# A decoder trunk on one core: fourteen pairs of up products instead of twelve, and the first down group ahead of the pairs

## The chip, the core and the metric

The kernel runs on one core of one Trainium2 chip. The metric is the device time of one execution in microseconds (us), shown as the median of several runs. A profile of one execution gives, for each engine, what it did and when: PE is TensorE (matmuls; PEld is its weight load), DVE is VectorE, ACT is ScalarE, POOL is GpSimd, and SP issues most of the DMAs.

## The reference, cut to what matters

Two layers of a decoder trunk for 512 positions of width 1024. In each layer three groups of heads (differential attention, a short convolution, RWKV-7 time mixing) share a norm, one input projection and one output projection; a squared-ReLU MLP follows. The change lies in the MLP alone:

```python
h = rms_norm(x, norm_mlp_g[l])
x = x + jnp.square(jax.nn.relu(h @ w_mlp_up[l])) @ w_mlp_down[l]    # 1024 -> 4096 -> 1024
```

## The kernel before, in words

**Layout.** Everything is transposed: a tile has 128 features as partitions and the 512 positions as its columns, so `x` is 8 tiles of 128x512. Weights come from HBM as `raw` tiles of 128x512 (four blocks of 128x128, 256 KB).

**Precision.** A product in fp32 precision is made of three passes of fp32r matmuls. Each operand is split into a high part (ACT casts it: `whi`, `mh`, `shi`, `thi`) and a low part (a subtraction of the two: `wlo`, `ml`, `slo`, `tlo`); the passes are hi by hi, hi by lo and lo by hi. So each tile that goes into a matmul first needs one cast on ACT and one subtraction with two inputs in SBUF on DVE or POOL.

**The MLP of a layer.** 32 groups of 128 up features. Up products come in two kinds:

- A single group, `up(i)`: 8 blocks by 3 passes, 24 matmuls of 512 columns, into one PSUM tile. Groups 0 to 2 are multiplied at the end of the mixing stage; `up` then only squares them.
- A pair, `two(i0, i1)`: two groups together by a scheme with 7 products of half size in place of 8. Each product is 12 matmuls of 256 columns, 84 in all. It needs 4 `raw` tiles, sums of them on DVE (`s1` to `s4`, line 1461), a cast (line 1455) and a subtraction (line 1456) for each of the 7 products, with five buffers in the ring of `shi` and `slo`. On the other side it needs sums of blocks of the normed input, `thi` and `tlo`.

The sums of blocks are made once a layer. `by_gain(j)` (ACT, line 1427) scales `x[j]` into `bn[j]`; `blocks(k)` takes `bn[k]` and `bn[k+4]`, makes four sums of 128x256 on DVE (lines 1433 to 1436) in two tiles `t[0]`, `t[1]`, casts each on ACT (`thi`, line 1440) and subtracts (`tlo`, line 1441). The tiles `t` take turns in four buffers, `s1` and `s2` for even `k`, `s3` and `s4` for odd `k`; so block 2 overwrites what block 0 used, and the pairs' own sums use the same four names.

Each up group is then squared by `square`: DVE scales the PSUM tile by the norm and cuts it at zero (`r`, line 1400), ACT squares it (`m`, line 1402), `kept` casts it (`mh`, ACT, line 1391) and subtracts on POOL (`ml`, line 1392). These are the "mids", in a ring of 10.

Down products, `down(h, js)`: a group `h` takes four mids and adds their part to `x[j]`; each `dn` tile is 12 matmuls of 512 columns, and DVE adds it to `x[j]` (line 1516). There are 8 groups of 8 tiles in a layer; the last layer does its last two in another way (`dnF`).

**Order.** The mixing stage is issued in an order that is written out by hand. The MLP is written as a plain program, and a scheduler puts it into an order for each engine; every engine then works through its own list strictly in order and waits for semaphores. The program's order before is: groups 0 to 7 single, with a `by_gain` pair and a `blocks` after each of the groups 4 to 7; the whole first down group; then twelve pairs, each followed by half a down group.

Of the kernel before, what the change touches and what calls it, by code (L numbers as in the profile page):

```python
# [10 lines left out]
F32 = mybir.dt.float32  # L11
# [5 lines left out]
ALU = mybir.AluOpType  # L17
# [7 lines left out]
NK = D // P  # L25
# [150 lines left out]
         "wp/wlo 01201201201201202102102102102102102102102102102102102102102102102102102102 ")  # L176
NG = NG_IN + NG_OUT + NG_UP + NG_DN

N_ONE = 8

WHOLE = 5
PT = 1
N_TWO = (NG_UP - N_ONE) // 2
MID = tuple(range(N_ONE)) + tuple(N_ONE + i + N_TWO * j for i in range(N_TWO) for j in range(2))

# [83 lines left out]
def tile_trunk(ctx: ExitStack, tc: tile.TileContext, xT, wts, prm_d, cst_d, lora_d, gup_d, lam_d, fin_d, out):  # L269
    nc = tc.nc  # L270
    act, dve, pool = nc.scalar, nc.vector, nc.gpsimd
# [27 lines left out]
    def psum(tag, bufs, name):  # L299
        return ps.tile([P, 512], F32, tag=tag, bufs=bufs, name=name)  # L300
# [56 lines left out]
    def mm3(out_ps, w, acts, n=NK):  # L357
        for _ in mm3_steps(out_ps, w, acts, n):
            pass
# [209 lines left out]
    for l in range(L):  # L569
# [807 lines left out]
        with ExitStack() as mx:  # L1377
# [42 lines left out]
            def by_gain(j):  # L1420

                if j == 0:
                    fp.tile([P, 8], F32, tag="pad0", name=f"pad0_{l}")
                bn[j] = fp.tile([P, 2, H], F32, tag="shi" if j < 4 else "slo", bufs=5, name=f"bn{l}_{j}")
                if j == 4:
                    fp.tile([P, 24], F32, tag="pad1", name=f"pad1_{l}")
                act.activation(bn[j].rearrange("p a s -> p (a s)"), x[j], AF.Identity, scale=pr[:, C_GMLP + j:C_GMLP + j + 1],
                               bias=none)

            def blocks(k):  # L1430
                b1, b2 = bn[k], bn[k + 4]
                t = [fp.tile([P, 2, H], F32, tag=f"s{2 * (k % 2) + i + 1}", name=f"t{l}_{k}_{i}") for i in range(2)]
                dve.tensor_tensor(t[0][:, 0], b1[:, 1], b1[:, 0], ALU.subtract)
                dve.tensor_tensor(t[0][:, 1], b2[:, 1], t[0][:, 0], ALU.subtract)
                dve.tensor_tensor(t[1][:, 0], b2[:, 1], b1[:, 1], ALU.subtract)
                dve.tensor_tensor(t[1][:, 1], b2[:, 0], t[0][:, 1], ALU.subtract)
                hi, lo = th[k] = [fp.tile([P, 4, H], F32R, tag=f"t{p}{k}", name=f"t{p}{l}_{k}") for p in ("hi", "lo")]
                for i in range(2):
                    u = slice(2 * i, 2 * i + 2)
                    act.copy(hi[:, u], t[i])  # L1440
                    dve.tensor_tensor(lo[:, u], t[i], hi[:, u].bitcast(F32), ALU.subtract)

            def two(i0, i1):

# [65 lines left out]
            def down(h, js):  # L1510

                g, k0 = h // 2, 4 * (h % 2)
                for j in js:
                    pt = psum("mm", 2, f"dn{l}_{h}_{j}")
                    mm3(pt, weights(wbase + NG_IN + NG_OUT + NG_UP + 8 * g + j, k0, k0 + 4), mids[4 * h:4 * h + 4], 4)
                    dve.tensor_tensor(x[j], pt, x[j], ALU.add)  # L1516
                    if h == 2 * N_KG - 1 and j < NK - LATE:
                        norm_tile(j, f"m{l + 1}")


            for i in range(N_ONE):
                up(i)
                if i >= N_ONE - 4:
                    k = i - N_ONE + 4
                    by_gain(k)
                    by_gain(k + 4)
                    blocks(k)
            down(0, range(NK))
            h, half = 1, 0
            for p in range(N_TWO):  # L1530
                two(N_ONE + p, N_ONE + N_TWO + p)
                if len(mids) >= 4 * h + 6 and h < 2 * N_KG - 2 * (l == L - 1):
# [75 lines left out]
```

## Time and profile before

| what | value |
|---|---|
| time, median of 3 runs | 1242.42 us (1241.35 to 1243.07) |
| span of the profiled execution | 1241.5 us |
| granted TensorE clock, mean | 0.998 |
| PE busy | 1230.0 us (99%) |
| DVE busy | 912.1 us (73%) |
| ACT busy | 675.0 us (54%) |
| POOL busy | 368.0 us (30%) |

Times below are us from the start of the profiled span. A row of the timeline has start, duration, engine, line, operation, the tile written and the tiles read, partitions by columns, and in brackets how long the engine had been idle before it and what ended that. PE's matmuls overlap, so the pace of a run of them is read from start to start, not from the duration of one. In a row of the groups the numbers behind the bar are the busy time of the group, the mean duration of one in ns, and the idle time before them with what ended most of it.

### The profile page before, as it was taken

The page shows a single profiled execution, that of the slowest core. Times are in us where ns is not written, and L with a number is a line of the kernel's source. Part 1 is how long each engine was busy: PE and PEld are TensorE (multiplying, and loading weights), DVE is VectorE, ACT ScalarE, POOL GpSimd, SP SyncE. Part 2 cuts the span into 40 slices and gives each one's busy share as a digit, 9 for nine tenths or more (in the row PEclk, how much of TensorE's full clock was granted, in tenths as well). Part 3 has the DMA queues.
Part 4 walks back from the last instruction along what each step waited for, and adds up shares of the span by engine and source line. Part 5 has one row for each costly group of instructions (what it writes and reads, how often), then busy time and mean ns, then how long its engine had stood idle before and what let it go on. Part 6 is the DMA issues. An engine that isn't in the chain of part 4 may idle for free.

```text
span 1241.5 us, 24974 instructions
## 1 busy us (share of the span) xinstructions
PE 1230.0 (99%) x9492; PEld 1055.0 (85%) x9492; DVE 912.1 (73%) x1776; ACT 675.0 (54%) x1410; POOL 368.0 (30%) x457
## 2 busy tenths in 40 slices
PE   9999999999999999999999999999999999999997
PEld 6888888888899998989887888888888999998987
DVE  6787888868767676765766777887687767676753
ACT  6785655548445454544464657464583445454542
POOL 1263637342311111111026355464231211111111
PEclk9999999999999999999999999999999999999999
DMA  6523324142433333321235244332433333333121
GB/s 216 163 87 99 105 96 111 53 153 85 136 102 98 107 94 106 99 85 44 69 106 164 79 118 119 89 83 73 158 102 120 102 102 98 107 94 107 55 68 68
DMA packets 84695, 127.90 MB, mean 103 GB/s; under 512 B 21472, under 2 KB 25568, under 8 KB 84576
## 3 DMA queue, kind: packets, MB, share of 16 engines
q1 hardware_dynamic: 83568, 125.64, 33.1%
q8 instruction: 74, 1.21, 0.4%
q10 hardware_dynamic: 1008, 0.68, 0.2%
q14 instruction: 45, 0.37, 0.1%
HBM read 117.11 MB, written 9.18 MB: 102 GB/s over the span
## 4 chain that ended last, share of the span: by engine, by line
PE 93%; ACT 2%; DVE 2%; DMA 1%; POOL 1%; issue 1%; ACTq 0%; POOLq 0%; DVEq 0%
PE dn L282 25%; PE pj L282 20%; PE pa L282 11%; PE po L282 8%; PE up L282 7%; PE pb L282 6%; PE dnF L282 4%; PE pc L282 3%; PE sc L282 1%; DMA raw<-wts 1%; PE ptt L287 1%; PE pg L282 1%; PE pyy L282 1%; PE pzw L282 1%; PE pst L282 1%
## 5 line engine op out<-in xcount | busy, mean ns | idle before, releaser
L1392 POOL TENSOR_TENSOR ml<-m,mh 128x512 fp32r<-128x512 f32 x64 | 108.9, 1716 | 481.0 <-ACT mh L1391 340.6
L344 ACT CAST whi<-raw 128x512 fp32r<-128x512 f32 x142 | 87.4, 619 | 162.4 <-PE dn L282 152.8
L282 PE MATMUL dn<-mh,whi 128*128 128x512 f32 x448 | 174.8, 390 | 0.1
L282 PE MATMUL dn<-ml,whi 128*128 128x512 f32 x448 | 174.6, 390 | 0.0
L282 PE MATMUL dn<-mh,wlo 128*128 128x512 f32 x448 | 174.5, 390 | 0.0
L683 POOL TENSOR_TENSOR wlo<-raw,whi 128x512 fp32r<-128x512 f32 x84 | 111.0, 1321 | 213.1 <-ACT whi L671 175.4
L282 PE MATMUL pj<-ahim,whi 128*128 128x512 f32 x392 | 156.7, 400 | 0.4 <-DVE vf L1278 0.4
L282 PE MATMUL pj<-ahim,wlo 128*128 128x512 f32 x392 | 156.4, 399 | 0.0
L282 PE MATMUL pj<-alom,whi 128*128 128x512 f32 x392 | 155.9, 398 | 0.0
L1516 DVE TENSOR_TENSOR x<-dn,x 128x512 f32<-128x512 f32 x112 | 77.3, 690 | 103.1 <-PE dn L282 103.1
L671 ACT CAST whi<-raw 128x512 fp32r<-128x512 f32 x142 | 87.6, 617 | 83.3 <-PE pj L282 25.1
L345 DVE TENSOR_TENSOR wlo<-raw,whi 128x512 fp32r<-128x512 f32 x142 | 115.0, 811 | 11.2 <-ACT whi L344 8.3
L282 PEld LDWEIGHTS dn<-mh,wlo 128*128 128x128 f32 x448 | 84.1, 188 | 17.8
L282 PEld LDWEIGHTS dn<-mh,whi 128*128 128x128 f32 x448 | 84.1, 188 | 17.5 <-issue 0.4
L282 PEld LDWEIGHTS dn<-ml,whi 128*128 128x128 f32 x448 | 84.1, 188 | 16.7
L1455 ACT CAST shi_p<-s 128x512 fp32r<-128x512 f32 x96 | 59.6, 621 | 70.1 <-PE pa L282 55.1
L282 PEld LDWEIGHTS pj<-ahim,whi 128*128 128x128 f32 x392 | 73.9, 188 | 14.1 <-issue 0.8
L282 PEld LDWEIGHTS pj<-alom,whi 128*128 128x128 f32 x392 | 73.9, 188 | 13.9 <-issue 0.5
L282 PEld LDWEIGHTS pj<-ahim,wlo 128*128 128x128 f32 x392 | 73.9, 188 | 13.8 <-issue 0.2
L1456 DVE TENSOR_TENSOR slo_p<-s,shi_p 128x512 fp32r<-128x512 f32 x96 | 67.9, 708 | 19.7 <-ACT shi_p L1455 17.2
L282 PE MATMUL pa<-tlo,shi_p 128*128 128x256 f32 x288 | 81.3, 282 | 0.0
L282 PE MATMUL pa<-thi,shi_p 128*128 128x256 f32 x288 | 81.2, 282 | 0.0
(414 smaller groups left out, 3208.1 us busy)
## 6 DMA issues: line engine op xcount, KB each, us to landing
raw<-wts SPq DMA_DIRECT2D x389, 256.0 KB, 2.7
qs<-dqhi SPq DMA_DIRECT2D x24, 128.0 KB, 3.7
ks<-dkhi SPq DMA_DIRECT2D x24, 128.0 KB, 3.7
x<-xT SPq DMA_DIRECT2D x8, 256.0 KB, 4.6
dqhi<-qhi SPq DMA_DIRECT2D x6, 256.0 KB, 3.4
dqlo<-qlo SPq DMA_DIRECT2D x6, 256.0 KB, 3.4
dkhi<-khi SPq DMA_DIRECT2D x6, 256.0 KB, 2.7
dklo<-klo SPq DMA_DIRECT2D x6, 256.0 KB, 3.5
```

Source lines behind the costliest of these rows:

```text
L282: ins = nc.tensor.matmul(*a, **k)
L287: ins = nc.tensor.transpose(*a, **k)
L344: act.copy(hi[:, :n], raw[:, :n])
L345: (pool if a and lean[0] else dve).tensor_tensor(lo[:, :n], raw[:, :n], hi[:, :n].bitcast(F32), ALU.subtract)
L671: yield act.copy(hi[:, k0:k1], raw[:, k0:k1])
L683: yield eng.tensor_tensor(lo[:, k0:k1], raw[:, k0:k1], hi[:, k0:k1].bitcast(F32), ALU.subtract)
L1392: pool.tensor_tensor(lo, m, hi.bitcast(F32), ALU.subtract)
L1455: act.copy(hi, src)
L1456: dve.tensor_tensor(lo, src, hi.bitcast(F32), ALU.subtract)
L1516: dve.tensor_tensor(x[j], pt, x[j], ALU.add)
```

## The change

The number of single groups, `N_ONE`, goes from 8 to 4, so the number of pairs a layer goes from 12 to 14. The low parts of the block sums, `tlo`, are subtracted on POOL instead of DVE. All eight `by_gain` come right behind group 3, and the first down group follows at once, two tiles at a time, with one `blocks` after each two; the pairs start behind it.

```diff
-N_ONE = 8
+N_ONE = 4
...
                     act.copy(hi[:, u], t[i])
-                    dve.tensor_tensor(lo[:, u], t[i], hi[:, u].bitcast(F32), ALU.subtract)
+                    pool.tensor_tensor(lo[:, u], t[i], hi[:, u].bitcast(F32), ALU.subtract)
...
             for i in range(N_ONE):
                 up(i)
-                if i >= N_ONE - 4:
-                    k = i - N_ONE + 4
-                    by_gain(k)
-                    by_gain(k + 4)
-                    blocks(k)
-            down(0, range(NK))
+            for j in range(NK):
+                by_gain(j)
+            for k in range(4):
+                down(0, (2 * k, 2 * k + 1))
+                blocks(k)
             h, half = 1, 0
             for p in range(N_TWO):
                 two(N_ONE + p, N_ONE + N_TWO + p)
```

The condition behind each pair (half a down group once the mids reach `4 * h + 6`) is the same. With four mids at the start instead of eight, it is first met after the third pair, so the first three pairs of a layer follow each other directly; before, the first half group came after the first pair.

What the scheduler makes of it shows at three places, all at the start of layer 0's MLP (names: layer, then group, block or down tile; the last number only tells tiles apart).

POOL, the low parts of the first mids. Before:

```order
L1392 TENSOR_TENSOR ml0_0_4157<-m0_0_4154,mh0_0_4156 128x512
L1392 TENSOR_TENSOR ml0_1_4165<-m0_1_4162,mh0_1_4164 128x512
L1392 TENSOR_TENSOR ml0_2_4173<-m0_2_4170,mh0_2_4172 128x512
L1392 TENSOR_TENSOR ml0_3_4218<-m0_3_4215,mh0_3_4217 128x512
L1392 TENSOR_TENSOR ml0_4_4263<-m0_4_4260,mh0_4_4262 128x512
```

Now:

```order
L1392 TENSOR_TENSOR ml0_2_4173<-m0_2_4170,mh0_2_4172 128x512
L1441 TENSOR_TENSOR tlo0_0_4286<-t0_0_0_4279,thi0_0_4285 128x512
L1441 TENSOR_TENSOR tlo0_0_4286<-t0_0_1_4280,thi0_0_4285 128x512
L1441 TENSOR_TENSOR tlo0_1_4338<-t0_1_0_4331,thi0_1_4337 128x512
L1441 TENSOR_TENSOR tlo0_1_4338<-t0_1_1_4332,thi0_1_4337 128x512
L1441 TENSOR_TENSOR tlo0_2_4390<-t0_2_0_4383,thi0_2_4389 128x512
L1392 TENSOR_TENSOR ml0_3_4218<-m0_3_4215,mh0_3_4217 128x512
```

Five subtractions of the block sums stand between the third and the fourth mid's low part, where there was nothing. In layer 1 there are four.

DVE, around the squaring of group 3 (`r0_3`). Before:

```order
L345 TENSOR_TENSOR wlo39_0_4288<-raw39_0_4285,whi39_0_4287 128x512
L1441 TENSOR_TENSOR tlo0_1_4340<-t0_1_1_4334,thi0_1_4339 128x512
L1441 TENSOR_TENSOR tlo0_2_4401<-t0_2_0_4394,thi0_2_4400 128x512
L1400 SCALAR_TENSOR_TENSOR r0_3_4213<-up0_3_4176,rsf0_4108 128x512
L1441 TENSOR_TENSOR tlo0_2_4401<-t0_2_1_4395,thi0_2_4400 128x512
L345 TENSOR_TENSOR wlo39_4_4306<-raw39_4_4303,whi39_4_4305 128x512
```

Now:

```order
L345 TENSOR_TENSOR wlo66_0_4243<-raw66_0_4240,whi66_0_4242 128x512
L1433 TENSOR_TENSOR t0_2_0_4383<-bn0_2_4226 128x256
L1434 TENSOR_TENSOR t0_2_0_4383<-bn0_6_4235,t0_2_0_4383 128x256
L345 TENSOR_TENSOR wlo68_0_4295<-raw68_0_4292,whi68_0_4294 128x512
L1435 TENSOR_TENSOR t0_2_1_4384<-bn0_6_4235,bn0_2_4226 128x256
L1400 SCALAR_TENSOR_TENSOR r0_3_4213<-up0_3_4176,rsf0_4108 128x512
L345 TENSOR_TENSOR wlo69_0_4315<-raw69_0_4312,whi69_0_4314 128x512
L1436 TENSOR_TENSOR t0_2_1_4384<-bn0_6_4235,t0_2_0_4383 128x256
L1433 TENSOR_TENSOR t0_3_0_4435<-bn0_3_4228 128x256
L1435 TENSOR_TENSOR t0_3_1_4436<-bn0_7_4237,bn0_3_4228 128x256
```

Two of block 2's sums (`t0_2_0`, `t0_2_1`) now stand ahead of `r0_3`. They write the buffers that POOL's first two `tlo` read, and wait for POOL.

PE, behind group 3. Before:

```order
L282 MATMUL up0_3_4176<-ahif0_7_4061,wlo37_4_4198 128x512
L282 MATMUL up0_4_4221<-ahif0_0_3851,whi38_0_4224 128x512
L282 MATMUL up0_4_4221<-alof0_0_3852,whi38_0_4224 128x512
L282 MATMUL up0_4_4221<-ahif0_0_3851,wlo38_0_4225 128x512
L282 MATMUL up0_4_4221<-ahif0_1_3880,whi38_0_4224 128x512
```

Now, the rows from the last of the first nine matmuls of `dn0_0_0` on (the nine take mids 0 to 2):

```order
L282 MATMUL dn0_0_0_4239<-mh0_2_4172,wlo66_0_4243 128x512
L282 MATMUL dn0_0_1_4259<-mh0_0_4156,whi67_0_4262 128x512
L282 MATMUL dn0_0_1_4259<-ml0_0_4157,whi67_0_4262 128x512
L282 MATMUL dn0_0_1_4259<-mh0_0_4156,wlo67_0_4263 128x512
L282 MATMUL dn0_0_1_4259<-mh0_1_4164,whi67_0_4262 128x512
L282 MATMUL dn0_0_0_4239<-mh0_3_4217,whi66_0_4242 128x512
L282 MATMUL dn0_0_1_4259<-ml0_1_4165,whi67_0_4262 128x512
L282 MATMUL dn0_0_0_4239<-ml0_3_4218,whi66_0_4242 128x512
```

PE goes from group 3 straight into the down group: 13 matmuls on mids 0 to 2, then one that needs `mh0_3`, one more, and then one that needs `ml0_3`. In layer 1 it is 15 instead of 13.

## The prediction

> **What bounds the kernel now.** First the page's busy times and the chain of waits, then the chain in the stretch where the change lies.
>
> ```profile
> PE 1230.0 (99%) x9492; PEld 1055.0 (85%) x9492; DVE 912.1 (73%) x1776; ACT 675.0 (54%) x1410; POOL 368.0 (30%) x457
> PE 93%; ACT 2%; DVE 2%; DMA 1%; POOL 1%; issue 1%; ACTq 0%; POOLq 0%; DVEq 0%
> 289.84 35.62 PE up L282 x157
> 325.46 21.77 PE dn L282 x96
> ```
>
> PE sets the end. At the start of layer 0's MLP it runs 157 up matmuls and then the 96 of the first down group without a wait: everything that DVE, ACT and POOL do there is hidden. So two questions decide: how much PE work goes, and whether PE now waits anywhere.
>
> **What PE saves.** From the timeline of PE, the starts of group 3, group 4, the first down tile, the first pair, and the down tile behind it:
>
> ```profile
> 298.10 0.39 PE L282 MATMUL up<-ahif,whi 128*128 128x512 f32 x1
> 303.54 0.39 PE L282 MATMUL up<-ahif,whi 128*128 128x512 f32 x1
> 325.30 0.39 PE L282 MATMUL dn<-mh,whi 128*128 128x512 f32 x1
> 347.07 0.28 PE L282 MATMUL pa<-ahif,shi_p 128*128 128x256 f32 x1
> 357.07 0.40 PE L282 MATMUL dn<-mh,whi 128*128 128x512 f32 x1
> ```
>
> A single group takes 303.54 - 298.10 = 5.44 us (24 matmuls, 0.227 each), a pair 10.00 us (84 matmuls, 0.119 each). A pair replaces two singles: 2 x 5.44 - 10.00 = 0.88 us. Two more pairs in each of two layers save 4 x 0.88 = **3.5 us**. The down products only move, and the bytes stay the same: two singles and one pair both load four tiles of 256 KB. That DVE loses the `tlo` gives nothing by itself, since DVE has 2% of the chain.
>
> **The new wait, what POOL costs.** Until now group 3's mid had four more single groups, 21.8 us, before the first down tile asked for it. Now the down group stands right behind group 3, at 303.54. After 13 matmuls on mids 0 to 2 (13 x 0.227 = 2.95, so at 306.5) PE needs `mh` of mid 3, and two matmuls later `ml` of mid 3. And POOL, which makes `ml`, gets five `tlo` ahead of it. Rows of groups and of POOL's timeline:
>
> ```profile
> L1392 POOL TENSOR_TENSOR ml<-m,mh x64: 1286/1644/4517, 293.3 to 1188.9; 128x512 fp32r<-128x512 f32 x64
> L1441 DVE TENSOR_TENSOR tlo<-t,thi 128x512 fp32r<-128x512 f32 x16 | 10.5, 677 | 0.0
> 568.19 2.55 POOL L1392 TENSOR_TENSOR ml<-m,mh 128x512 fp32r<-128x512 f32 x2 [16.86 <-ACT mh L1391]
> ```
>
> `tlo` took 0.68 us on DVE. The trace has no `tlo` on POOL, but `ml` has the same form: alone, two in 2.55 us, 1.27 each; at worst 4.5. What makes the difference is DVE:
>
> ```profile
> 308.57 4.28 POOL L1392 TENSOR_TENSOR ml<-m,mh 128x512 fp32r<-128x512 f32 x1 [4.52 <-ACT mh L1391]
> 311.62 0.67 DVE L1400 SCALAR_TENSOR_TENSOR r<-up,rsf 128x512 f32<-128x512 f32 x1
> 312.22 1.18 DVE L345 TENSOR_TENSOR wlo<-raw,whi 128x512 fp32r<-128x512 f32 x1
> 359.62 3.39 POOL L1392 TENSOR_TENSOR ml<-m,mh 128x512 fp32r<-128x512 f32 x2 [28.84 <-ACT mh L1391]
> 360.68 1.19 DVE L345 TENSOR_TENSOR wlo<-raw,whi 128x512 fp32r<-128x512 f32 x1
> ```
>
> From 308.57 DVE ran subtractions back to back, and POOL's operation ended only after DVE came to `r` at 311.62, which reads PSUM; the `wlo` behind that took 1.18 instead of 0.68. At 360.68 it is DVE that waits: its `wlo` ends 0.56 us after POOL's first operation, and POOL's second comes after it. I read this as turns: an operation with two inputs in SBUF excludes the other engine's, a waiting one goes in next, and a string without a gap keeps the other out. POOL's turn, net, is 1.27 less a lead of about 0.12, so 1.15 us. The Trainium skill says the same in "SBUF — State Buffer", section "SBUF: two separate sides": DVE and GpSimd share a port pair that is locked for a whole instruction, and the loser blocks fully; the trace agrees (1.18 against 0.68).
>
> **The wait in layer 0, step by step.** Paces from the timelines, start to start:
>
> ```profile
> 290.69 0.82 ACT L1427 ACTIVATE bn<-x,none,prm 128x512 f32<-128x512 f32 x1 [0.22 <-DVE none L1418]
> 291.41 0.62 ACT L1402 ACTIVATE m<-r 128x512 f32<-128x512 f32 x1
> 292.64 0.61 ACT L1391 CAST mh<-m 128x512 fp32r<-128x512 f32 x1
> 293.15 0.62 ACT L344 CAST whi<-raw 128x512 fp32r<-128x512 f32 x1
> 299.34 0.41 DVE L1435 TENSOR_TENSOR t<-bn,bn 128x256 f32<-128x256 f32 x1
> 299.68 0.68 DVE L1400 SCALAR_TENSOR_TENSOR r<-up,rsf 128x512 f32<-128x512 f32 x1
> 300.28 0.68 DVE L345 TENSOR_TENSOR wlo<-raw,whi 128x512 fp32r<-128x512 f32 x1
> ```
>
> On ACT a `bn` takes 0.72, a cast or square 0.52; on DVE an operation of 512 columns 0.60, of 256 columns 0.34. Until 290.69 nothing changes.
>
> - ACT: eight `bn` and six casts or squares stand ahead of mid 2's square: 8 x 0.72 + 6 x 0.52 = 8.9, to 299.6. Square, `whi`, `mh`: 1.7, so `mh` of mid 2 is there at 301.3.
> - POOL: `ml` of mid 2 to 302.8, the first `tlo` to 304.1. DVE stands since about 301.7: its `t0_2_0` overwrites what that `tlo` reads. Behind it in DVE's list wait `wlo68` and `r0_3`, and for `r0_3` ACT and then PE.
> - Turns: DVE `t0_2_0` (0.4); POOL second `tlo` (1.15); DVE three operations (1.3), which reaches `r0_3` at 307.0; POOL third `tlo`, to 308.2; DVE `wlo69` and two `t` (1.3); POOL fourth, to 310.6; DVE four (1.7); POOL fifth, to 313.4; DVE `s1` (0.6); POOL `ml` of mid 3, to 315.2.
> - ACT: `r0_3` ends at 307.6; square, `shi`, `mh` make 309.3.
>
> PE stands from 306.5 to 309.3, does two matmuls (0.45), and stands to 315.2: **8.2 us** in all. Behind it PE's list is only late; the down group's weights and the pair's operands use the time.
>
> **Layer 1.** There POOL has four `tlo` ahead, and PE 15 matmuls. Group 3 starts here at 907.50 and ends at:
>
> ```profile
> 907.50 0.39 PE L282 MATMUL up<-ahif,whi 128*128 128x512 f32 x1
> 912.95 0.39 PE L282 MATMUL up<-ahif,whi 128*128 128x512 f32 x1
> ```
>
> PE runs out at 912.95 + 15 x 0.227 = 916.35. Mid 2 can't be scaled before group 2 ends (907.7); `r` to 908.4, then on ACT a `bn`, the square, a `bn` and the cast give `mh` at 910.9. Turns: `ml` to 912.3; DVE two `wlo` (1.1); POOL first `tlo` to 914.6; DVE `t0`, `r` at 915.0; POOL to 916.2; DVE two `wlo` and three `t` (2.2); POOL to 919.5; DVE one `t` (0.5); POOL to 921.1; DVE two `t` (0.8); `ml` of mid 3 to 923.1. PE stands 923.1 - 916.35 - 0.45 = **6.3 us**.
>
> Bounds for both: with no exclusion, POOL's operations one behind the other, 301.4 + 7 x 1.27 = 310.3 and 911.0 + 6 x 1.27 = 918.6, so 3.4 and 1.8 us, 5.2 together. Above, with every POOL operation at 4.5 us, it would be 26 and 21; but the strings that DVE has here are at most 2.2 us long, so I take the turns: 14.5.
>
> **TensorE's clock.** A gap of that length has a second price. PE's first rows, its last one, and two windows around the end:
>
> ```profile
> 1.22 4.18 PE L282 MATMUL idle<-zero 128*128 128x512 bf16 x10 [1.22 <-DVE zero L394]
> 5.05 0.58 PE L282 MATMUL pj<-ahim,whi_s 128*128 128x512 f32 x1
> 1235.18 0.66 PE L282 MATMUL prbF<-eyeF,rloF 128*128 128x128 f32 x4
> 1233.00:1236.00 3.00, 1.89 (x12) 1.56 (x12) 1.22 (x8) 1.14 (x5) 0.44 (x1) 1.00 0.75 261
> 1236.00:1239.00 3.00, 0.00 (x0) 0.00 (x0) 1.73 (x6) 0.25 (x1) 1.41 (x2) 0.70 0.66 229
> ```
>
> PE's last work ends at 1235.84 after some thin us, and in the next window the granted clock is down to 0.70. At the start ten matmuls took 3.83 us where 2.27 is the warm pace, 1.6 us lost. So each gap costs nothing more or about 1.6; I count one: **+1.6**. The Trainium skill, "TensorE: Matmul & The Clock Gate", section "Part 1: The HAM clock gate", halves the clock after one idle window of about 3.4 us; by it both gaps pay, which is a rival below. The end of this trace agrees as far as it goes.
>
> **The three pairs in a row.** DVE has to make a pair's operands in a pair's time: 12 operations of 0.60 and 6 of 0.34, 9.2 of 10.00 us. Rows for two pairs that follow each other at the end of layer 1, and for loads:
>
> ```profile
> 1166.11 0.28 PE L282 MATMUL pa<-ahif,shi_p 128*128 128x256 f32 x1
> 1176.11 0.28 PE L282 MATMUL pa<-ahif,shi_p 128*128 128x256 f32 x1
> 1186.17 0.40 PE L282 MATMUL dnF<-mh,whi 128*128 128x512 f32 x1
> 303.50:325.30 21.80, 21.80 (x98) 18.02 (x97) 21.75 (x34) 14.61 (x26) 10.15 (x4) 1.00 0.41 125
> ```
>
> They keep 10.00. Three take 12 tiles of 256 KB in 30 us on SP's queue, 105 GB/s, under the 125 that the last row shows with PE full. The ring of five, filled during the down group, covers the rest: I cost it at 0, and without that cover at two `ml` turns a pair, 9.2 + 2.3 - 10.0 = 1.5, times six pairs 9.
>
> **Sum.** -3.5 + 8.2 + 6.3 + 1.6 = +12.6. The profiled 1241.5 becomes 1254.1; the median of the runs lies 0.9 above the profiled span, so **1255.0**.
>
> **The rivals.**
>
> - *No exclusion:* POOL's operations keep 1.27 us, PE stands 5.2 us: -3.5 + 5.2 = +1.7, 1244.1. For it: the median `ml` is only 1.64. Against it: the 1.18 and 4.28 above.
> - *The clock falls in both gaps:* 1.6 more, 1256.6. For it: both gaps are longer than the thin stretch at the end. Against it: two matmuls divide each.
> - *Hidden after all, faster:* the mid arrives before PE asks, and 3.5 us stay: 1238.9. The place is POOL between 301.4 and 307; seven operations fit only under 0.8 us each. Against it: of 64 `ml` none took less than 1.286.
> - *DVE becomes the bound in the three pairs as well:* up to 9 more, 1259 to 1264. For it: 9.2 of 10.00 leaves little. Against it: the tail pairs keep pace, with a lighter DVE, and PE's new gap gives DVE a lead.
>
> **How the numbers follow.** Two runs of this kernel can be told apart from about 0.2%, 2.5 us. Chances: forecast 0.46, the clock twice 0.20, no exclusion 0.17, DVE bound 0.12, hidden 0.05. The forecast's own range is 1250 to 1258 (no drop of the clock or two, a string more or less). For 8 in 10 the range reaches down towards the rival without exclusion and up to the first of the DVE case: 1246 to 1260. Faster is the hidden case, 0.05; same takes 0.10 of the case without exclusion; slower is the rest, 0.85.
>
> **What would show it.** In the profile after: PE idle behind group 3 in both layers, released by POOL `ml`, 5 to 8 us each; `tlo` on POOL at over 1.27 us; DVE waiting for POOL ahead of `t` (line 1433); the first three pairs still at 10.00 each; a slice with a granted clock below 1 at these two places. I'm wrong if PE passes from group 3 to the down group without a gap, or if the gap ends by ACT's `mh` and not by `ml`.

## The result, and the profile after

The changed kernel takes **1264.42 us** (median of 5 runs, 1263.25 to 1267.75) against 1242.42 before: a ratio of 1.0179, 95% interval 1.0166 to 1.0192, so 22.0 us slower. I had forecast 1255.0, 12.6 slower, with a range of 1246 to 1260. The sign was right, the size was not, and the time lies outside the range. The profiled execution has a span of 1264.2 us, 22.7 over that of before; it took 1266.02, the second longest of the five, whose mean granted clocks lie between 0.988 (this one) and 0.993 (the shortest), so the price of the clock below is that of this execution.

The page of the changed kernel: busy times, and the shares of the chain of waits.

```profile
PE 1238.0 (98%) x9636; PEld 1065.1 (84%) x9636; DVE 939.2 (74%) x1808; ACT 685.4 (54%) x1434; POOL 383.6 (30%) x473
PE 88%; DVE 5%; ACT 3%; issue 2%; DMA 1%; POOL 1%; ACTq 0%; POOLq 0%; DVEq 0%
```

PE had 93% of the chain and now has 88%; DVE went from 2% to 5%. The busy time of PE grew although it has less work, mostly since matmuls at half clock count as longer. The groups of instructions of the same kernel show on what PE waits, and what a `tlo` takes on POOL:

```profile
L282 PE MATMUL dn<-ml,whi 128*128 128x512 f32 x448 | 177.7, 397 | 3.4 <-POOL ml L1392 3.4
L282 PE MATMUL dn<-mh,whi 128*128 128x512 f32 x448 | 177.6, 397 | 8.9 <-ACT mh L1391 7.7 <-DVE x L1516 1.2
L282 PE MATMUL pa<-thi,shi_p 128*128 128x256 f32 x336 | 95.9, 285 | 3.7 <-ACT p L1484 3.6
L1441 POOL TENSOR_TENSOR tlo<-t,thi 128x512 fp32r<-128x512 f32 x16 | 23.4, 1480 | 5.0 <-ACT thi L1440 4.9
```

So PE waits for `mh` (7.7 us), for `ml` (3.4), once for DVE's addition `x` (1.2), and in the pairs (3.6). The last two I had not counted. Now the place of the change, PE's timeline in layer 0 and then in layer 1:

```profile
305.68 0.40 PE L282 MATMUL dn<-mh,whi 128*128 128x512 f32 x1
311.92 0.80 PE L282 MATMUL dn<-mh,whi 128*128 128x512 f32 x1 [5.84 <-ACT mh L1391]
312.51 0.63 PE L282 MATMUL dn<-ml,whi 128*128 128x512 f32 x1
314.77 0.80 PE L282 MATMUL dn<-ml,whi 128*128 128x512 f32 x1 [1.63 <-POOL ml L1392]
...
927.53 0.39 PE L282 MATMUL dn<-mh,wlo 128*128 128x512 f32 x1
929.75 0.73 PE L282 MATMUL dn<-mh,whi 128*128 128x512 f32 x2 [1.83 <-ACT mh L1391]
932.23 0.80 PE L282 MATMUL dn<-ml,whi 128*128 128x512 f32 x1 [1.74 <-POOL ml L1392]
...
935.59 0.42 PE L282 MATMUL pa<-alof,shi_p 128*128 128x256 f32 x1
937.23 0.79 PE L282 MATMUL dn<-mh,whi 128*128 128x512 f32 x1 [1.22 <-DVE x L1516]
```

Start to start, less the 0.23 of one matmul, PE stands 6.0 + 2.0 = 8.0 us in layer 0, and 2.0 + 1.9 + 1.4 = 5.3 in layer 1 (the last against 0.21, a pair's matmul at half clock). The durations of 0.63 to 0.80 behind the gaps are the clock. The windows of PE show it; the columns behind the length are PE's busy time and its instructions, the granted clock, the share of the DMA engines and GB/s:

```profile
305.71:309.13 3.42, 0.37 (x2) 1.00 0.01 2
309.13:319.37 10.24, 5.82 (x13) 0.50 0.22 63
319.37:322.78 3.41, 3.41 (x17) 1.00 0.35 116
926.94:930.35 3.41, 1.58 (x7) 1.00 0.32 91
930.35:940.59 10.24, 7.28 (x18) 0.50 0.22 73
978.14:981.55 3.41, 1.35 (x11) 1.00 0.22 77
981.55:984.97 3.42, 3.42 (x18) 0.50 0.00 0
```

Ahead of the program's end the clock fell three times, twice for 10.24 us and once for 3.41. The third drop lies in the pairs of layer 1. DVE and POOL of the changed kernel in layer 0, ahead of mid 3:

```profile
303.50 1.50 DVE L1433 TENSOR_TENSOR t<-bn 128x256 f32<-128x256 f32 x1 [2.46 <-POOL tlo L1441]
305.03 1.40 DVE L1434 TENSOR_TENSOR t<-bn,t 128x256 f32<-128x256 f32 x1
306.36 1.75 DVE L345 TENSOR_TENSOR wlo<-raw,whi 128x512 fp32r<-128x512 f32 x1
308.04 1.48 DVE L1435 TENSOR_TENSOR t<-bn,bn 128x256 f32<-128x256 f32 x1
309.44 0.68 DVE L1400 SCALAR_TENSOR_TENSOR r<-up,rsf 128x512 f32<-128x512 f32 x1
310.64 0.41 DVE L1436 TENSOR_TENSOR t<-bn,t 128x256 f32<-128x256 f32 x1
...
302.17 7.06 POOL L1441 TENSOR_TENSOR tlo<-t,thi 128x512 fp32r<-128x512 f32 x5
311.94 2.77 POOL L1392 TENSOR_TENSOR ml<-m,mh 128x512 fp32r<-128x512 f32 x1 [2.71 <-ACT mh L1391]
```

During POOL's first `tlo` DVE waits for the buffer that it reads (2.46 us). While POOL works off the other four (1.41 each), DVE gets in **one** operation for each of them: sums that take 0.41 alone take 1.40 to 1.50, and `wlo` 1.75 instead of 0.68. So `r` of group 3 starts at 309.44, and `mh` and `ml` follow from there. Once POOL is empty, DVE's string runs at full speed and holds the single `ml` of mid 3 out (2.77 us).

Where the time went by stage, from the starts of the first matmuls (profiled executions, us):

| stage | before | after | difference |
|---|---|---|---|
| singles fewer, pairs more: PE's work | | | -3.5 |
| first down group, layer 0 | 21.77 | 32.59 | +10.8 |
| first down group, layer 1 (after: without two matmuls of a pair) | 22.13 | 30.68 | +8.5 |
| first three pairs, layer 0 | 30.00 | 32.45 | +2.4 |
| first three pairs, layer 1 | 30.00 | 34.37 | +4.4 |
| each later half down group, layer 0 | 10.93 | 11.04 | 11 x 0.11, and 0.34 in the three at the end: +1.5 |
| each later half down group, layer 1 | 10.93 | 10.93 | 0 |
| mixing stages and the start | | | -1.7 |

The sum is +22.4, against 22.7 for the spans. What made the mixing stages shorter I haven't traced.

### The profile page after: what moved, and what is told of

Read it like the earlier page. It is cut to its first block, busy times and chain, and to the rows that moved or that the text cites. A ratio compares the mean times of both kernels' runs of the same rounds, so it can differ in the third digit from the quotient of the medians.

```text
span 1264.2 us, 25354 instructions
## 1 busy us (share of the span) xinstructions
PE 1238.0 (98%) x9636; PEld 1065.1 (84%) x9636; DVE 939.2 (74%) x1808; ACT 685.4 (54%) x1434; POOL 383.6 (30%) x473
## 4 chain that ended last, share of the span: by engine, by line
PE 88%; DVE 5%; ACT 3%; issue 2%; DMA 1%; POOL 1%; ACTq 0%; POOLq 0%; DVEq 0%
PE dn L282 24%; PE pj L282 21%; PE pa L282 12%; PE po L282 8%; PE pb L282 6%; PE dnF L282 4%; PE pc L282 3%; DMA raw<-wts 1%; PE sc L282 1%; PE up L282 1%; PE ptt L287 1%; PE pg L282 1%; PE pyy L282 1%; DVE slo_p L1456 1%; PE pzw L282 1%
## 5 line engine op out<-in xcount | busy, mean ns | idle before, releaser
L1392 POOL TENSOR_TENSOR ml<-m,mh 128x512 fp32r<-128x512 f32 x64 | 101.4, 1598 | 484.2 <-ACT mh L1391 325.4
L282 PE MATMUL dn<-mh,whi 128*128 128x512 f32 x448 | 177.6, 397 | 8.9 <-ACT mh L1391 7.7
L282 PE MATMUL dn<-ml,whi 128*128 128x512 f32 x448 | 177.7, 397 | 3.4 <-POOL ml L1392 3.4
L344 ACT CAST whi<-raw 128x512 fp32r<-128x512 f32 x126 | 77.7, 618 | 162.9 <-PE dn L282 152.0
L671 ACT CAST whi<-raw 128x512 fp32r<-128x512 f32 x142 | 87.7, 617 | 81.6 <-PE pj L282 25.0
L345 DVE TENSOR_TENSOR wlo<-raw,whi 128x512 fp32r<-128x512 f32 x126 | 104.0, 827 | 11.7 <-ACT whi L344 9.8
L1455 ACT CAST shi_p<-s 128x512 fp32r<-128x512 f32 x112 | 69.5, 620 | 76.1 <-PE pa L282 58.9
L282 PE MATMUL pa<-thi,shi_p 128*128 128x256 f32 x336 | 95.9, 285 | 3.7 <-ACT p L1484 3.6
L282 PE MATMUL pa<-tlo,shi_p 128*128 128x256 f32 x336 | 95.4, 284 | 0.0
L282 PE MATMUL pa<-thi,slo_p 128*128 128x256 f32 x336 | 94.8, 282 | 0.0
L1456 DVE TENSOR_TENSOR slo_p<-s,shi_p 128x512 fp32r<-128x512 f32 x112 | 77.8, 696 | 20.2 <-ACT shi_p L1455 17.8
```

What stands on the lines that cost most here:

```text
L282: ins = nc.tensor.matmul(*a, **k)
L344: act.copy(hi[:, :n], raw[:, :n])
L345: (pool if a and lean[0] else dve).tensor_tensor(lo[:, :n], raw[:, :n], hi[:, :n].bitcast(F32), ALU.subtract)
L671: yield act.copy(hi[:, k0:k1], raw[:, k0:k1])
L1392: pool.tensor_tensor(lo, m, hi.bitcast(F32), ALU.subtract)
L1455: act.copy(hi, src)
```

## The experiments

Times are medians beside runs of the kernel before on the same chip (1242.2 to 1242.6). Stages are read from the profiled execution as in the table.

### Which part of the change costs what

Each part of the change alone, put into the kernel before. The low parts of the block sums on POOL:

```diff
-                    dve.tensor_tensor(lo[:, u], t[i], hi[:, u].bitcast(F32), ALU.subtract)
+                    pool.tensor_tensor(lo[:, u], t[i], hi[:, u].bitcast(F32), ALU.subtract)
```

> The kernel before, with the low parts of the block sums on POOL and nothing else changed. Theory (the subtraction on POOL costs only where PE asks for the fourth mid at once): four single groups, 21.8 us, lie between, so PE waits nowhere, and the time is that of before within 1 us (1242 to 1243.5). Rival (the turns of DVE and POOL slow DVE so much that it is late for any work): gaps of PE show behind groups 4 to 7 too, 1246 or more.

Measured: 1251.40, ratio 1.0074 (1.0059 to 1.0089). My theory of that moment fell, and the rival held: 9.0 us, although four singles stood behind group 3. PE's timeline in layer 0, in group 4:

```profile
314.50 0.39 PE L282 MATMUL up<-alof,whi 128*128 128x512 f32 x1
317.28 0.50 PE L282 MATMUL up<-ahif,wlo 128*128 128x512 f32 x1 [2.40 <-DVE wlo L345]
```

Not `ml` is late but `wlo`, DVE's share of the weights: over both layers PE waits 5.7 us for `wlo` and 1.5 for `x`. With POOL's `tlo` in turn, DVE can't feed PE in time, even where nothing asks for mid 3 early.

The new order alone, with eight singles and `tlo` on DVE:

```diff
-                if i >= N_ONE - 4:
-                    k = i - N_ONE + 4
-                    by_gain(k)
-                    by_gain(k + 4)
-                    blocks(k)
-            down(0, range(NK))
+            for j in range(NK):
+                by_gain(j)
+            for k in range(4):
+                down(0, (2 * k, 2 * k + 1))
+                blocks(k)
```

> The kernel before (eight single groups, low parts of the block sums on DVE), with the order changed alone: the blocks stand beside the first down group. Theory: mids 0 to 3 are long ready, so PE doesn't wait behind the singles; DVE has the block sums (16 of 0.34 and 8 of 0.60, 10.2 us) and 16 operations of 0.60 of the down group in 21.8 us, so the first pair starts with less in hand; 1242 to 1244. Rival (the order alone costs, since the first pair needs thi and tlo right behind the down group): the first pair takes over 10.5 us in both layers, 1245 or more.

Measured: 1243.87, ratio 1.0010 (1.0001 to 1.0020). The order alone costs 1 to 2 us, as the theory had it: one gap of 1.8 us (start to start) in layer 1, nearly nothing in layer 0.

Four singles alone, in the old order:

```diff
-N_ONE = 8
+N_ONE = 4
```

> The kernel before, with four single groups instead of eight and nothing else changed: the blocks stand beside groups 0 to 3, the low parts on DVE. Theory: four singles don't give DVE and ACT time for the blocks, so PE waits 2 to 5 us in each layer around group 3 and the first down tiles; the three pairs in a row lose 1 to 2.5 us in each layer; -3.5 + 7 + 3.5 = +7, 1249, with a drop of the clock (about 2 us) where the wait is in one piece. Rival (the fourteen pairs are as good as free, and all the loss comes from POOL and the new order): 1239 to 1243.

Measured: 1260.43, ratio 1.0146 (1.0131 to 1.0162). More than twice what I expected. In layer 1 PE stands 4.3 us in one piece ahead of group 3, for ACT's `whi`: ACT works there almost without a pause at its eight `bn`, the squares and casts, and DVE waits for the `bn`. In layer 0 it stands 1.6 and 1.3 us around group 3; the clock falls in both layers, and the three pairs lose 2.3 and 2.6. It is the largest single part; the three parts alone cost more than 28 us in sum, against 22.0 for the whole change, so they don't simply add up. The new order makes four singles cheaper, as the next kernel shows: the changed one with `tlo` back on DVE, so four singles and the new order together.

```diff
-                    pool.tensor_tensor(lo[:, u], t[i], hi[:, u].bitcast(F32), ALU.subtract)
+                    dve.tensor_tensor(lo[:, u], t[i], hi[:, u].bitcast(F32), ALU.subtract)
```

> The changed kernel with one part undone: the low parts of the block sums are subtracted on DVE again. Theory (mid 3 comes late because DVE, ahead of r of group 3, does one operation for each of POOL's five): POOL has only ml in its queue, DVE reaches r of group 3 at about 304.8 instead of 309.4, mh is there at 306.2 and ml at 307.7, so PE stands about 1.5 us in layer 0 instead of 8.0, and under 1 us instead of 5.1 in layer 1; no window of the clock is idle long enough, so the granted clock stays at 1.0 there. DVE has 4.8 us more to do beside the down group, so the three pairs lose as much as now or more (5 to 8 us). In all 1241 to 1249. Rival (mid 3 is late because only 13 matmuls stand between group 3 and it, whoever subtracts): the gaps stay at 5 us or more in both layers and the time at 1260 or more.

Measured: 1253.45, ratio 1.0086 (1.0070 to 1.0101), between the two expectations. PE's waits in the first down group shrink from 8.0 to 3.0 us (the gaps are 1.38 and 2.06 start to start) and from 5.3 to 1.2, the pairs lose 2.5 and 2.0. The profiled execution is the shortest of four (1250.30), and its clock doesn't drop ahead of the program's end; the others have lower mean clocks. So moving `tlo` to POOL costs 11.0 of the 22.0 us here, and 9.0 in the kernel before: it is dear in either order.

### Is it DVE's time?

Nobody subtracts `tlo`; ACT writes the tile:

```diff
-                    pool.tensor_tensor(lo[:, u], t[i], hi[:, u].bitcast(F32), ALU.subtract)
+                    act.copy(lo[:, u], t[i])
```

> The changed kernel with tlo written by an ACT cast of the sums instead of a subtraction, which leaves the low part's arithmetic out there. Neither DVE nor POOL subtracts. Theory (what remains at 1253.4 with tlo on DVE is the time that DVE lacks beside the down group): DVE has 4.8 us less a layer than there, so the waits in the first down group shrink to 0 to 1.5 us a layer and the three pairs lose 0 to 1.5 us: 1241 to 1247. Rival (ACT is the bound there: eight bn, thi and the casts): with 4.2 us more on ACT the waits stay as with tlo on DVE or grow, 1253 or more.

Measured: 1247.64, ratio 1.0038 (1.0023 to 1.0052), 0.6 us above the theory's range and far below the rival's. The first down groups take 23.40 and 22.85, 1.6 and 0.7 over before, though ACT has more to do. ACT isn't the bound; relieving DVE by 9.6 us in all against `tlo` on DVE gives 5.8. About half of that is clock: at a mean clock of 0.998 the two kernels stand at 1250.30 and at 1247.44 to 1247.75. But the three pairs still take 32.40 and 32.90: their loss has another cause than the subtraction of `tlo`. (The block sums themselves are still on DVE here.)

Idle matmuls to keep PE busy, to price the clock, failed as a measurement:

```diff
+            warm = psum("at", 2, f"warm{l}")
+            for _ in range((34, 20)[l]):
+                pe.matmul(warm, cent, acts[0][0], start=True, stop=True)
```

> The changed kernel with idle matmuls (34 in layer 0, 20 in layer 1; 512 columns, 0.227 us each, so 7.7 and 4.5 us) on PE behind group 3, into a PSUM tile that nobody reads. They fill the wait and take no longer than it. Theory (PE's gaps cost twice: the wait and then the half clock, which held for three windows of 3.41 us): mid 3 comes as late as before, the granted clock stays at 1.0 at both places, and 2.9 + 3.6 = 6.5 us come back: 1258. Rival (the half clock costs next to nothing because PE only waits in those windows): 1263 to 1266.

Measured: 1278.71, ratio 1.0294 (1.0276 to 1.0311). The scheduler gave the kernel another order: nine operations of the pair now stand ahead of DVE's addition of a down tile, so PE gets a new wait of 6.8 us for `x` behind the one for mid 3, and the clock falls there. What it does show: counted from the end of group 3, `ml` of mid 3 lets PE go on after 10.9 us in layer 0, where it was 11.8. Work on PE doesn't bring it forward by more than that.

### Why three pairs in a row take longer

DVE relieved of three of seven `slo` in these pairs:

```diff
+                    if i0 < N_ONE + 3 and name in ("p6", "p3", "p4"):
+                        act.copy(lo, src)
+                    else:
+                        dve.tensor_tensor(lo, src, hi.bitcast(F32), ALU.subtract)
-                    dve.tensor_tensor(lo, src, hi.bitcast(F32), ALU.subtract)
```

> The changed kernel, with three of the seven slo (products p6, p3, p4) of the first three pairs of each layer made by an ACT cast instead of a DVE subtraction, which leaves the low part's arithmetic out there (the tile holds the whole value). DVE has 1.8 us less in each of these pairs, 7.4 instead of 9.2 of 10.00. Theory (DVE, with turns against POOL's ml, bounds the three pairs, and the raw tiles come late because DVE frees their buffers late): the three pairs come back to 30.0 to 30.5 us in both layers, the third drop of the clock goes, and the time falls by 5.5 to 7 to about 1258. Rival (the loads on SP's queue bound the three pairs by themselves, 4 tiles in 10 us): the waits stay, 1262 to 1265.

Measured: 1259.06, ratio 1.0139 (1.0124 to 1.0154). The pairs come down to 30.4 and 31.0 us and the third drop of the clock is gone; the median is 5.4 us lower. So DVE is in it, but by what? In the changed kernel's layer 0 PE and DVE show a late load and POOL's turns:

```profile
359.34 0.28 PE L282 MATMUL pc<-alof,shi_p 128*128 128x256 f32 x1
361.13 0.39 PE L282 MATMUL pa<-thi,shi_p 128*128 128x256 f32 x1 [1.51 <-ACT p L1484]
...
348.45 1.79 DVE L1461 TENSOR_TENSOR s<-raw,raw 128x512 f32<-128x512 f32 x1
350.50 1.45 DVE L1461 TENSOR_TENSOR s<-raw,s 128x512 f32<-128x512 f32 x1
355.37 0.69 DVE L1461 TENSOR_TENSOR s<-raw,raw 128x512 f32<-128x512 f32 x1 [1.29 <-DMA raw<-wts]
...
348.40 2.99 POOL L1392 TENSOR_TENSOR ml<-m,mh 128x512 fp32r<-128x512 f32 x2 [29.52 <-ACT mh L1391]
```

Two kernels take away one of the two each, both on top of the one with `tlo` by ACT, where PE's wait in layer 0's pairs (us in total, times, longest) is:

```profile
PE pa L282 <- ACT p L1484: 1.4, 1, 1.4
```

Without POOL's `ml` in these pairs:

```diff
+                if N_ONE <= len(mids) < N_ONE + 6:
+                    act.copy(lo, m)
+                else:
+                    pool.tensor_tensor(lo, m, hi.bitcast(F32), ALU.subtract)
-                pool.tensor_tensor(lo, m, hi.bitcast(F32), ALU.subtract)
```

> The kernel with tlo by an ACT cast, and the ml of the six mids of the first three pairs of each layer by an ACT cast too, which leaves their low part out. Theory (in these pairs DVE's own 9.2 of 10.00 us would do, and what is too much are POOL's turns, two ml a pair that hold DVE for about 1 us each): the three pairs come back to 30.0 to 30.7 us in both layers (32.4 and 32.9 with the ml on POOL), 4 to 5 us less in all, 1243 to 1244. Rival (DVE's own work, in the order given, or late raw tiles bind them): they stay over 32 us, 1247 to 1248.

And with a seventh buffer for the pairs' loads:

```diff
-                    t = fp.tile([P, 4, P], F32, tag="sraw", bufs=6, name=f"raw{n}_{i}_{a}")
+                    t = fp.tile([P, 4, P], F32, tag="sraw", bufs=7, name=f"raw{n}_{i}_{a}")
```

> The kernel with tlo by an ACT cast, with seven buffers for the pairs' raw tiles instead of six (the first 32-byte pad falls away for it). Theory of the turns: the raw tiles are late only because DVE frees them late; the pairs change by less than 0.7 us a layer, 1246 to 1248. Rival (the loads bind, since a buffer comes free too late for a transfer of 2.6 us): the wait of DVE for raw goes and the pairs come back to 30 to 30.7 us, 1243 to 1244.

Measured: 1245.19 (ratio 1.0019, 1.0010 to 1.0028) and 1245.95 (1.0029, 1.0018 to 1.0041) against 1247.64. From the first pair's start to the end of the half group behind the third (30.00 + 11.04 and + 10.93 without a loss), with `tlo` by ACT it is 43.43 and 43.83 us; without the turns 42.28 and 42.16; with seven buffers 42.35 and 42.25. So each takes away about half of the loss of 2.4 and 2.9, and neither theory holds alone. The wait for `p` (1.4 us in layer 0, 1.9 in layer 1) is gone or down to 0.4 with either change, so I read it as one chain: POOL's turns make DVE late, DVE frees the load buffers late, and the load that comes late then holds DVE. Both changes at once were not run. The seventh buffer also moves the tiles: a pair alone takes 10.06 there, and the half groups 10.99 and 10.89, so by its own paces its loss is 1.2 in each layer. That rest, 1.2 us a layer in both kernels, I haven't traced.

### Why layer 0's later down groups are slower

The order is the same in both layers, but the tiles lie elsewhere: SBUF places are given in the order of first use, and with fewer singles the fourth weight buffer is first used behind the buffers of `shi` in layer 0, in layer 1 ahead of them, as before. Given that place by hand:

```diff
                 if j == 0:
+                    fp.tile([P, 4, P], F32, tag="raw4", name=f"place_raw{l}")
+                    for k in ("whi4", "wlo4"):
+                        fp.tile([P, 4, P], F32R, tag=k, name=f"place_{k}{l}")
```

> The changed kernel with three tiles of the fourth weight buffer (raw, whi, wlo) given their place in SBUF ahead of the buffers of shi and slo, as the kernel before has it in both layers and the changed one in layer 1 only; order and work are the same. Theory (in layer 0 the later half down groups take 11.04 instead of 10.93 us because tiles lie elsewhere): they come back to 10.93, 11 times 0.11 and 0.34 at the end, 1.6 us less; waits and clock stay: about 1262.8. Rival (the slower pace of the down products comes from the earlier gaps or from the order): they stay at 11.04, 1264.4.

Measured: 1263.36, ratio 1.0165 (1.0148 to 1.0181). The half groups of layer 0 are back at 10.93, and the three at the end at 32.68. The median moved by 1.1 us, within its spread; the verdict rests on the stages, which agree to 0.01 us over all eleven.

### Is there a version with more pairs that wins?

Six singles in the old order:

```diff
-N_ONE = 8
+N_ONE = 6
```

> The kernel before with six single groups and thirteen pairs, nothing else changed. PE saves 2 x 0.88 = 1.8 us. Theory (two singles and the down group behind the fourth mid, 32.7 us, still hide blocks and mids, and two pairs in a row lose under 1 us): 1240.5 to 1242. Rival (two pairs in a row already bind DVE, and the blocks one group earlier make PE wait): 1243 to 1248.

Measured: 1252.34, ratio 1.0079 (1.0064 to 1.0094). The first down group takes 3.1 and 4.3 us more than before, with waits for ACT's casts (`whi` 2.4 us in layer 0), whose list waits for DVE, and a drop of the clock in layer 1. The two pairs lose 0.5 in each layer, and the later half groups take 11.04 and 11.00 instead of 10.93.

The changed order, low parts on DVE, split so that no two pairs follow each other:

```diff
             for k in range(4):
-                down(0, (2 * k, 2 * k + 1))
+                down(0, (k,))
                 blocks(k)
...
                 two(N_ONE + p, N_ONE + N_TWO + p)
+                if p < 2:
+                    down(0, (4 + 2 * p, 5 + 2 * p))
```

> The changed kernel with the low parts on DVE and the first down group split: four tiles ahead of the first pair, two behind it, two behind the second, so that no two pairs follow each other. Theory (three pairs in a row take DVE more than their 30 us, and down tiles between them give it time): the second and third pair come back to 10.0 us, 2 to 4 us less than with the low parts on DVE alone; but block sums now have 10.9 us less in front of the first pair, so that pair loses 1 to 4 us: 1246 to 1254. Rival (the first wait, for mid 3, is all that counts): 1252 to 1255.

Measured: 1254.77, ratio 1.0098 (1.0080 to 1.0116). The second and third pair are back at 10.00 (the second of layer 1: 10.93), but the wait for `ml` of mid 3 in layer 1 grows to 2.8 us, and the clock falls in both layers. Nothing is gained against 1253.45.

Six singles in the new order, low parts on DVE, tiles placed as before:

```diff
-N_ONE = 4
+N_ONE = 6
...
-                    pool.tensor_tensor(lo[:, u], t[i], hi[:, u].bitcast(F32), ALU.subtract)
+                    dve.tensor_tensor(lo[:, u], t[i], hi[:, u].bitcast(F32), ALU.subtract)
```

> Six single groups and thirteen pairs in the new order, low parts on DVE, tiles placed as in the kernel before. Theory (PE's work ahead of the first pair has to cover DVE's): between eight singles in this order (1243.9) and four (1253.4 less 1.6 for the places): the two singles more give mids 0 to 3 time, so no wait for mid 3; DVE is late in the down group by 1 to 3 us a layer and two pairs lose 0.5: 1243 to 1248. Rival (the wait for mid 3 was all, and order plus places now hide everything): 1239.5 to 1242, faster than before.

Measured: 1246.99, ratio 1.0030 (1.0020 to 1.0041). The same with lighter pairs:

```diff
-                dve.tensor_copy(p5, pb)
+                act.copy(p5, pb)
...
-                act.copy(c1, pa)
-                dve.tensor_tensor(c1, c1, p5, ALU.add)
+                dve.tensor_tensor(c1, pa, p5, ALU.add)
```

> The same, and in each pair p5 is copied by ACT instead of DVE, and c1 is added by DVE straight from PSUM (ACT's copy falls away): DVE has 0.34 us less in a pair, and one operation less with both inputs in SBUF. Theory: 0.3 to 1 us less than without, all of it in the first two pairs and in the down group before them; 1242 to 1247. Rival (pairs aren't bound by DVE): the same time within 0.3 us.

Measured: 1246.95, ratio 1.0033 (1.0021 to 1.0045): nothing. The wait is elsewhere. Without the lighter pairs, PE's waits in layer 1's first down group (us in total, times, longest) are one:

```profile
PE dn L282 <- DVE x L1519: 2.0, 1, 2.0
```

In layer 0 it is the same with 1.2. DVE's addition of a down tile is late, and only two PSUM banks serve the down tiles. So four banks:

```diff
-                    pt = psum("mm", 2, f"dn{l}_{h}_{j}")
+                    pt = psum(*(("at", 2) if h == 0 and j % 4 > 1 else ("mm", 2)), f"dn{l}_{h}_{j}")
```

> Six single groups in the new order, tiles placed as before, low parts on DVE, and the first down group takes turns in four PSUM banks instead of two (those of the attention are free there), so that PE can run four tiles ahead of DVE's additions instead of two. Theory (PE's gap of 1.6 and 2.4 us there is DVE's late x, and what DVE lacks can be made up later): the gaps go, PE's gain of 1.8 us shows against a loss of 1 to 2 us in the pairs: 1241.5 to 1244.5. Rival (what DVE lacks only moves into the first pair): 1245.5 to 1247.

Measured: 1241.62, ratio 0.9992 (0.9983 to 1.0001), 5.4 us less than with two banks. The first down group takes 21.77 in both layers, without a wait, where it took 23.69 and 24.06; some 2 of the 5.4 us look like clock: the one with two banks at a mean of 0.998 took 1244.94, and most others, slower, had 0.996 or 0.997. With the lighter pairs on top:

> Six single groups with four PSUM banks for the first down group, and the lighter pairs (p5 copied by ACT, c1 added straight from PSUM). What is left there against 20.00 and 10.93 us are 0.5 us in each layer's two pairs and 0.3 and 0.7 in the half group behind them. Theory (DVE's backlog): 0.34 us less DVE work a pair and one operation less that POOL can hold up take most of it away: 0.5 to 1.2 us less, 1240.4 to 1241.2. Rival (as without the four banks, where the lighter pairs gave nothing): 1241.3 to 1242.

Measured: 1241.40, ratio **0.9987 (0.9979 to 0.9996)**: faster than the kernel before by 0.13%, about 1.1 us against the 1.8 that PE saves; the two pairs still take 20.47. It is small; its interval just leaves out 1, that of the kernel without the lighter pairs doesn't, and it is the best of several tries, so whether it wins is at the edge of what these runs can tell. Of this kernel's groups, the row of the down products has no wait left:

```profile
L282 PE MATMUL dn<-mh,whi 128*128 128x512 f32 x448 | 174.7, 390 | 0.0
```

And fourteen pairs with all of it:

> Four single groups and fourteen pairs in the new order with all of it: low parts on DVE, places as before, four banks, lighter pairs. PE saves 3.5 us. Theory (mid 3 can't come in time behind only 13 to 16 matmuls, and three pairs in a row bind DVE): 2 to 3 us of wait in layer 0, 0 to 1.5 in layer 1, 0.5 to 2 in each layer's three pairs: 1241.5 to 1246. Rival (the banks were what was missing): 1239 to 1240.5.

Measured: 1250.56, ratio 1.0059 (1.0047 to 1.0071). PE again waits for `mh` and `ml` of mid 3 (1.38 and 2.06 start to start in layer 0, 2.71 in layer 1), and the three pairs lose 2.4 and 2.5. So the gain of 3.5 us wasn't had in this order with any of these means. My reading, which no run isolates, is that four singles give DVE and ACT too little time ahead of mid 3.

## Why the prediction was wrong, point by point

Two terms of the sum failed. The price of the clock was 1.6 us for one drop, and the drops cost 8.1. The three pairs in a row were put at 0, and they cost 5.1. The two waits, the largest terms, came out near their size, but for the first of them by luck: the step that gave it was wrong.

| term | forecast | measured | from |
|---|---|---|---|
| PE's work | -3.5 | -3.5 | 21.76 us of singles less, two pairs of 10.00 more, in each layer |
| wait in layer 0 | 8.2 | 8.0 | 6.0 + 2.0 |
| wait in layer 1 | 6.3 | 5.3 | 2.0 + 1.9 + 1.4 |
| clock | 1.6 | 8.1 | 2.8 + 3.6 + 1.7 |
| three pairs in a row | 0 | 5.1 | 2.45 + 2.67 |
| places in SBUF | not seen | 1.5 | 11 x 0.11 + 0.34 |
| the rest of the program | 0 | -2.0 | start, mixing, 0.36 of wait that layer 1's first down group had before |

The measured column is that of the profiled execution. It sums to 22.5, for a span that grew by 22.7. The clock's share is what the first down groups took beyond their 21.77 and the waits (32.59 - 21.77 - 8.0; 30.68 - 21.77 - 5.3), and half of the 3.42 us window in the pairs.

**PE's work: right**, to 0.1 us.

**The wait, layer 0 and layer 1: the sizes right, the step of the turns wrong.** I let a string of three or four DVE operations pass in one turn, so that `r0_3` came at 307.0, or 306.4 with the 0.6 us by which this execution is ahead. It came at 309.44, because DVE got one operation for each `tlo`. In return POOL was through its five `tlo` by 309.2, where I had its fifth at 313.4. The two errors cancel, which is luck: the end of the wait lies 0.2 us from the forecast. By my own sign of being wrong, a gap that ends by `mh` and not by `ml`, the step failed: 6.0 of the 8.0 us end by `mh`, where I had 2.8, and 2.0 by `ml`, where I had 5.4. In layer 1 I had one wait of 6.3 for `ml`; it was 2.0 for `mh`, 1.9 for `ml` and 1.4 for `x`. The cause named, POOL's `tlo` against DVE, stands: the gap falls to 3.0 with `tlo` on DVE and to 1.0 without any. My reading was also too narrow. I priced POOL only where PE asks for mid 3, and the kernel with nothing but `tlo` on POOL lost 9.0 us, most of it to a late `wlo`. My sentence that freeing DVE of the `tlo` gives nothing was right for the wrong reason: the move didn't free DVE, since a sum beside a `tlo` on POOL took 1.40 to 1.50 instead of 0.41.

**The clock: the price right, the count wrong.** I had 1.6 for one drop. A drop of one window costs that: six singles in the new order and the same with lighter pairs have the same gap of 2.40 us in layer 1, and only in the second did the clock fall, for one window; its first down group takes 25.63 against 24.06, 1.57 more. The matmul behind the gap and PE's windows around it, first without the lighter pairs, then with them:

```profile
931.28 0.47 PE L282 MATMUL dn<-mh,whi 128*128 128x512 f32 x1 [2.01 <-DVE x L1519]
927.12:930.54 3.42, 2.15 (x10) 1.00 0.24 77
930.54:933.95 3.41, 2.67 (x12) 1.00 0.42 141
...
933.92 0.47 PE L282 MATMUL dn<-mh,whi 128*128 128x512 f32 x1 [2.02 <-DVE x L1518]
931.44:934.85 3.41, 1.40 (x7) 1.00 0.35 112
934.85:938.26 3.41, 3.41 (x9) 0.50 0.68 205
```

But a gap isn't one drop. In layer 0 the clock stayed at half for three windows, in layer 1 too, and a third time in the pairs. The rival of two drops was still far too low. The Trainium skill, "TensorE: Matmul & The Clock Gate", section "Part 1: The HAM clock gate", has the free-running window of about 3.4 us, and the drops of the changed kernel last 3.41 or three times that; its condition, a whole idle window, doesn't agree, as the last section here shows.

**The three pairs in a row: wrong.** I cost them at 0, with 9 as the bound without the ring as cover; they cost 5.1, between the two. The rows from the end of layer 1 did not carry over: two pairs there keep 10.00, but two at the start of a layer, in the kernels with six singles, lose 0.5, and three lose more. The estimate of 1.5 for a pair without cover was nearer than the cover I believed in. POOL's turns were in it, the load buffers that DVE frees late were not. The measured time lies at the top of the rival in which DVE becomes the bound there, 1259 to 1264, but that rival had 9 us from the pairs; the rest of the way came from the clock.

**Places in SBUF: missed.** The order of the instructions, on which I had built the prediction, doesn't show them.

## What to carry to other kernels

Where DVE and POOL both have operations with two inputs in SBUF, the work that moves from DVE to POOL still takes DVE's time: count each moved operation against both, at every place where the first one feeds PE, not only where the moved result is asked for. Before a change takes PE work out of a stretch, add up what DVE must do there; if it's the larger sum, expect the gain to be lost, and look at buffers that let PE run ahead: here two more PSUM banks gave 5.4 us, more than the 3.5 that fewer matmuls could give. And price a gap on PE with its clock: whether and how long it drops depends on how the gap lies in the windows.

## What I had not expected of the hardware

**The clock goes by a window's idle share, not by a gap's length.** In all traces of this study, with their windows of 3.413 us, every window ahead of the program's last 12 us that began at full clock and had 1.76 us or more of PE idle (by the matmuls' modelled ends) was followed by half clock, and every one with 1.72 or less by full clock. So a gap of 2.4 us drops the clock or doesn't, by where it falls, as the two kernels with six singles show. The Trainium skill's section named above puts the drop behind one idle window; here half a window was enough. The window nearest the edge that kept the clock, from the kernel with only `tlo` on POOL, with the window behind it, is shown here; the changed kernel's at 926.94, shown above with 1.58 us busy, lies on the other side.

```profile
313.19:316.60 3.41, 1.70 (x8) 1.00 0.02 5
316.60:320.01 3.41, 2.73 (x12) 1.00 0.46 139
```

At half clock it comes back only behind a window that is nearly full: 0.73 us idle kept it down, 0.50 let it up. So a second gap soon after the first keeps it low, which is how layer 0 came to three windows. Whether it drops differs between executions of one kernel: with `tlo` on DVE, four of them took 1250.30, 1252.95, 1253.94 and 1254.83 us at mean clocks of 0.998, 0.997, 0.996 and 0.994. At the end of the program, where PE does thin matmuls of few columns, windows with less idle time (1.07 us) dropped it too.

**Between DVE and POOL it goes one for one.** While both have work waiting, an operation of DVE with two inputs in SBUF took 1.40 to 1.75 us, one POOL operation long, and POOL's `tlo` came every 1.41 us, where an `ml` alone took 1.30. A single POOL operation that meets a running string of DVE waits for the string's end (2.77 us). The Trainium skill, "SBUF — State Buffer", section "SBUF: two separate sides", says that whoever starts first has the ports and the other blocks; the trace agrees, and adds who comes next: with work waiting on both sides the two engines take turns, one operation each.

**PE's pace depends on where tiles lie.** The same down matmuls came at 0.227 us or at up to 0.24 start to start, by the places of other tiles alone: 0.11 us for 48 matmuls, shown by the kernel with the places of before. With a seventh load buffer, which moves the tiles again, a pair took 10.06 us and the half groups 10.99 and 10.89. Which place disturbs which is open.
